# Two-layer hybrid decoder trunk on one core: the low half of the mix reloaded through GpSimd's queue, and the second convolution's taps placed behind the gate's first subtraction

## The chip, the cores and the metric

The kernel runs on one core of a Trainium2 chip. A core has a matrix engine (TensorE, PE in the profile), VectorE (DVE), ScalarE (ACT), GpSimd (POOL) and SyncE (SP); each works through its own list of instructions in order, and the lists are tied together by semaphores. Transfers are started by SP, ACT or POOL and carried out by 16 DMA engines that the core's queues share. The metric is the device time of one execution in microseconds (us), as the median of several runs. A profile is taken of one further execution.

## The reference

Two equal layers on x of 512 tokens by 2048 features. Cut to what matters here:

```python
def _layer(x, norm_g, w_in, conv_w, conv_b, ..., w_out):
    h = _rmsnorm(x, norm_g)
    proj = h @ w_in
    (cv_h, cv_b, cv_c, cv_g, sb_q, sb_k, sb_v, sb_g,
     gl_q, gl_k, gl_v, gl_g, gl_lr) = jnp.split(proj, split_points, axis=-1)
    y_conv = _short_conv(cv_h, cv_b, cv_c, conv_w, conv_b) * silu(cv_g)   # 512 columns
    y_sb = stick-breaking attention of 8 heads * silu(sb_g)               # 1024 columns
    y_gla = rmsnorm(gated linear attention of 4 heads) * silu(gl_g)       # 512 columns
    mix = jnp.concatenate([y_conv, y_sb, y_gla], axis=-1)
    return x + mix @ w_out

def _short_conv(h, b_gate, c_gate, w, bias):
    u = c_gate * h
    y = causal depthwise convolution of u with 3 taps (w)
    return b_gate * (y + bias)
```

All is float32.

## The kernel before, in words

**Products.** A float32 operand is held as a high and a low float16 half, and a product is three float16 products (high by high, high by low, low by high). The halves of the weights are made on the core: a group of 256 weight columns is fetched as float32 (2 MB, tile `st`, two buffers), ScalarE finds its largest square (L383, the "junk" pass, once for each MB), GpSimd takes the maximum over the partitions (L399, tile `wgm`), VectorE makes the scale of it in a few one-column steps (L402 to L417, tiles `wq`, `ws`, `wu`), ScalarE rounds to the high half (`wh`, L454, or L507) and VectorE subtracts for the low half (`wl`, L461, or L508).

**Groups.** A list of weight groups gives the order of the products in each layer: six for the linear attention, four for convolution 0 (h, c, g, b), sixteen for the attention (v, g, q, k of four head pairs), four for convolution 1, and eight output groups of `w_out`. `weights()` takes the next group of the list. At its call the group two further on is fetched by GpSimd's queue (`fetch`, L362), as soon as a `st` buffer is free, that is when the low halves of the group before it are made. With the first and a later matmul of the group it also has the next group's junk pass and its halves placed ("hooks").

**Quick groups.** Some groups are multiplied as 2 by 2 blocks with seven products instead of eight (`project_quick`). It has four partial results in two PSUM banks, `pa` and `pb` in one, `pd` and `pf` in the other (`za`, `zb`, `zd`, `zf` where they are read), which are copied out by ScalarE (L809, L813, L816) and combined by VectorE (L810, L817 to L828), while later products add into the same places. Each product is 24 matmuls of 128 by 256 (L794). The right sides are sums of blocks of the input, tiles `s` (a pair of 2 MB tiles made ahead); the seventh weight part stands in tiles of its own, `w7h` and `w7l`.

**The mix.** The results of the three branches are split in a high and a low half and stored in DRAM (`mixd`), 256 KB for each 128 columns and both halves. The buffers that hold the two halves for the output products are the ones that held the sums `s`, so the reload can begin only when the last quick group of the input, conv g 1, is done with them: the high half (`mix[0]`, an `m` tile) goes over the sums that the fourth of its seven products reads last, the low half (`mix[1]`, the other `m` tile) over those that the product with `wt1` reads. `mixload` issues the reload in three slices of 256, 768 and 512 KB for each half. It is called in `conv_in(1)`, which stands for conv h 1 and conv c 1; `conv_out(1)` then takes conv g 1 (the gate) and conv b 1. After the gate, `weight_ratio` finds one common scale and rescales the halves in place, the high half on ScalarE (L1201), the low half on VectorE (L1202), seven instructions each. Output group 0 (L712, L713, L714) reads them; L714 is the matmul that reads the low half.

**The last attention heads** run in between: their scores are turned by DMA transposes on SP (`th<-za`, L1301), and their products with the values are L1317, 18 matmuls a head. They are called `values(0)` and `values(1)` below. The taps of convolution 1 are two products (L1216), two scalings (L1226) and four shifted multiply-adds (L1228) on VectorE.

**Order.** The program is written in one sequence, and a scheduler that simulates the engines sets the order in each engine's list, with priorities for the weight work. `order(a, b)` only places a behind b.

Of the kernel before, what the change touches and what calls it, by code (L numbers as in the profile page):

```python
# [11 lines left out]
ALU = mybir.AluOpType  # L12
# [31 lines left out]
def hybrid_trunk(ctx, tc, x, norm_g, w_in, conv_w, conv_b, sb_qn_g, sb_kn_g,  # L44
# [132 lines left out]
    def pcol(k, i):  # L177
        return par[:, base[k] + i:base[k] + i + 1]
# [16 lines left out]
    def order(a, b):  # L195
        tc.add_manual_dep(a.ins, b.ins.name, mybir.DependencyInfo(
            mybir.DependencyClass.NoSync, mybir.DependencyReason.DATA), reason="order")
# [248 lines left out]
        else:  # L446
            V.tensor_scalar(wh[:, ks, :GW], staged[0][h][:, ks, :GW], scales[0], None, ALU.mult)

    hooks, lastmm, ksq, added = [], [None], [], [None]

    def whi(i, h):
        wh = wpool.tile([P, HK, GX], F16, tag="wh", name=nm("wh"))
# [83 lines left out]
    def weights():  # L536

        i = cursor[0]
        cursor[0] += 1
        held = names[i][:2] == "v " or names[i] == "conv h 1"  # L540
        if i + 2 < len(specs) and not held:
            with tc.high_priority():
                fetch(i + 2)
        assert not hooks

        def first(mm):
            squares(i + 1, mm)
            if held:
                with tc.high_priority():
                    fetch(i + 2, added[0])  # L550

        if i and i + 1 < len(specs):
            hooks.extend([first, lambda mm: parts_of(i + 1, mm)])
        return loaded.pop(i)
# [130 lines left out]
    for l in range(depth):  # L685
# [89 lines left out]
                parts.extend([a[:, 2 * n], a[:, 2 * n + 1]] for n in range(2))  # L775
            return sums_of((xh, xl), parts, lambda t: [wk([P, HK, P], tag) for tag in ("zw", "zw", "g")])

        def project_quick(src, sums, y, cols, end=None):

            (w11, wT2, w22, wT3, w21, wt1, wT4), u = weights()  # L780
            banks = [bank(psp, "p") for _ in range(3 if end else 2)]
            pa, pb, pd, pf = ([bk[:, n * GW:(n + 1) * GW] for bk in banks for n in range(2)] if not end else
                              [banks[i][:, n * GW:(n + 1) * GW] for i, n in ((0, 0), (0, 1), (1, 0), (2, 0))])
            a11, a12, a22 = ([a[:, 2 * r:2 * r + 2, c::2, :] for a in src] for r, c in ((0, 0), (0, 1), (1, 1)))
            s_, a21_22, a12_s, a11_21 = sums

            def prod(o, w, a, start, stop=False):
                for t in range(1 if cols else 2):
                    for kk in range(HK):
                        for i, (p_, q_) in enumerate(((0, 0), (0, 1), (1, 0))):  # L790
                            st_ = start and t == kk == i == 0
                            en = stop and kk == HK - 1 and i == 2
                            if cols:
                                mm = T.matmul(o, w[q_][:, kk, :], a[p_][:, :, kk, :], start=st_, stop=en,  # L794
                                              skip_group_check=True)
                            else:
                                mm = T.matmul(o[:, t * P:(t + 1) * P], a[p_][:, t, kk, :], w[q_][:, kk, :], start=st_,  # L797
                                              stop=en, skip_group_check=True)
                            if start and t == kk == 0 and i == 2 and o is pa:
                                hook(mm)  # L800
                return mm

            y11, y12, y21, y22 = (
                y[:, c, r * GW:(r + 1) * GW] if cols else y[:, 2 * r:2 * r + 2, c * P:(c + 1) * P]
                for r in range(2) for c in range(2))
            za, zb, zd, zf = (a if cols else a.rearrange("p (t c) -> p t c", c=P) for a in (pa, pb, pd, pf))
            prod(pa, w11, a11, True)
            hook(prod(pb, wT2, s_, False))
            S.activation(y12, za, AF.Copy)  # L809
            V.tensor_tensor(y21, zb, y12, ALU.subtract)  # L810
            prod(pf, w22, a12_s, True)
            prod(pd, wT3, a11_21, end is not None)
            S.activation(y22, zd, AF.Copy)  # L813
            prod(pa, w21, a12, False)
            prod(pb, wt1, a21_22, False, True)
            S.activation(y11, za, AF.Copy)  # L816
            V.tensor_tensor(y12, zb, y12, ALU.subtract)  # L817
            V.tensor_tensor(y22, y12, y22, ALU.subtract)
            if end:
                V.tensor_tensor(y12, zf, y12, ALU.add)  # L820
                end(u, None)
                prod(pd, wT4, a22, False, True)
                end(u, zd)
                return
            lastmm[0] = prod(pd, wT4, a22, False, True)
            V.tensor_tensor(y12, zf, y12, ALU.add)
            yield 0, u
            V.tensor_tensor(y21, zd, y21, ALU.subtract)  # L828
            yield 2, u

        def project(cols, dst):

            if cursor[0] not in quick:
                return project_cols() if cols else project_toks(xh, xl)
            y = dst()
            for _, u in project_quick((xh, xl), insums, y, cols):
                pass
            if cols:
                return [y[:, c, :] for c in range(2)], u
            return [y[:, 2 * b:2 * b + 2, :].rearrange("p a c -> p (a c)") for b in range(2)], u  # L840
# [13 lines left out]
                ps.append(o)  # L854
                yield t, o, u

        def project_gate(mx=None, logistic=False, room=None):

            g = []

            def dst():
                g.append(room or wk([P, 2, seq], "g"))
                return g[0]

            ps, u = project(True, dst)
            quick_ = bool(g)
            g = dst() if not quick_ else g[0]
            top = sm(2, "gtop2") if mx is not None else None
            for c in range(2):
                y = g[:, c, :]  # L870
                if logistic:
                    a = wk([P, seq], "ga") if quick_ else y
                    tables.append(S.activation(a, ps[c], AF.Sigmoid, scale=u))
                    for b in tables[-9:-1]:
                        order(tables[-1], b)
                    if mx is None:
                        V.scalar_tensor_tensor(y, ps[c], u, a, ALU.mult, ALU.mult)
                    else:
                        V.tensor_tensor_reduce(y, ps[c], a, u, 0.28, ALU.mult, ALU.max, top[:, c:c + 1])
                    continue  # L880
                S.activation(y, ps[c], AF.Copy, scale=u)
                a = wk([P, seq], "ga")
                S.activation(a, y, AF.Abs)
                S.activation(a, a, AF.Exp, scale=-1.0)
                S.activation(a, a, AF.Ln, bias=1.0)
                V.scalar_tensor_tensor(a, y, 0.0, a, ALU.min, ALU.subtract)
                tables.append(S.activation(a, a, AF.Exp))
                if mx is None:
                    V.tensor_tensor(y, y, a, ALU.mult)
                else:  # L890
                    V.tensor_tensor_reduce(y, y, a, 1.0, 0.28, ALU.mult, ALU.max, top[:, c:c + 1])
            if mx is not None:
                V.tensor_tensor(mx, top[:, :1], top[:, 1:], ALU.max)
            return g, u
# [29 lines left out]
        def mixload():  # L924

            mix.extend(halves("m", 1 - l))
            for ks in (slice(0, 2), slice(4, 10), slice(12, KT)):
                assert all(k in split for k in range(ks.start, ks.stop))
                for i in range(2):
                    order(nc.sync.dma_start(mix[i][:, :, ks, :], mixd[l][:, i * NT:(i + 1) * NT, ks, :]), lastmm[0])  # L930

# [272 lines left out]
        def conv_in(j, then=lambda: None):  # L1206
# [5 lines left out]
            then()  # L1212
            uc = wk([P, 2, seq], "raw", 1) if j else wk([P, 2, seq], "zw")
            ps, u = project(True, lambda: uc)
            for c in range(2):
                V.scalar_tensor_tensor(uc[:, c, :], ps[c], u, hb[:, c, :], ALU.mult, ALU.mult)  # L1216
            if j:
                mixload()
            y = wk([P, 2, seq], "kT")
            for c in range(2):  # L1220
                ch = 2 * j + c

                def w_(i):
                    return pcol("cw", (l * 3 + i) * 4 + ch)

                V.tensor_scalar(y[:, c, :], uc[:, c, :], w_(2), pcol("cb", l * 4 + ch), ALU.mult, ALU.add)  # L1226
                for d in (1, 2):
                    V.scalar_tensor_tensor(y[:, c, d:], uc[:, c, :seq - d], w_(2 - d), y[:, c, d:], ALU.mult, ALU.add)  # L1228
            then()
            return y, None if j else hb  # L1230

        def conv_out(j, y, room, then=lambda: None):

            g, u = project_gate(logistic=j == 1, room=room)
            V.tensor_tensor(y, y, g, ALU.mult)
            bound = sm(2, "cm")

# [273 lines left out]
```

## Time and profile before

| | |
|---|---|
| median of 3 runs | 1637.63 us (1636.24 to 1638.91) |
| profiled execution, its own time | 1649.88 us |
| span of its profile | 1648.1 us, granted TensorE clock 0.995 |
| busy: PE, DVE, ACT, POOL | 1617.6, 1444.3, 1197.5, 269.8 us |
| DMA traffic | 235.99 MB, 143 GB/s on the mean |

The span runs from the first to the last instruction on the core; the execution's own time has some 2 us around it. A row of the timeline has the start and the duration in us, the engine, the line of the code, the operation, the tile written and the tiles read (out<-in), and in brackets how long the engine had stood idle before it and which tile, made by whom, ended that. Rows of equal instructions are drawn together (x18). SPq is SP's sequencer, which issues transfers. The profiled execution took 12 us longer than the median of the timed runs.

### The profile page before, as it was taken

Reading aid. Unit: us, or ns where it says so; the run is one execution under the profiler, and the core shown is the slowest. Engines: PE = TensorE matmul, PEld = TensorE weight load, DVE = VectorE, ACT = ScalarE, POOL = GpSimd, SP = SyncE. Lnnn points to the kernel's source line nnn. Section 1 sums busy time; section 2 is a strip of 40 time slices with the busy share of each in tenths; the row PEclk is TensorE's granted clock in tenths of the full one; section 3 lists DMA queues with packets and bytes.
Section 4 is the critical chain, followed back from the end, with each engine's and each line's share of the span. In section 5 each row is a group of like instructions: output and inputs, shape, how many; then the busy total and the mean of one; then the engine's idle time right before and its main releaser. Section 6 shows DMA issues by size and latency. Waiting matters only on the chain.

```text
span 1648.1 us, 42250 instructions
## 1 busy us (share of the span) xinstructions
PE 1617.6 (98%) x18202; PEld 1356.3 (82%) x18202; DVE 1444.3 (88%) x2417; ACT 1197.5 (73%) x1771; POOL 269.8 (16%) x300
## 2 busy tenths in 40 slices
PE   7999999999999999999999999999999999989998
PEld 5757768989898967899985768689899998748998
DVE  7989989989898978888698898998989898868896
ACT  8668877968687876666766788787878777755573
POOL 0122021211212121111112112121112112110110
PEclk9999999999999999999999999999999999999999
DMA  7154345476767678445634345456686967693441
GB/s 260 57 125 150 82 124 124 109 158 159 149 158 152 154 159 237 135 156 171 209 99 112 96 116 141 117 135 140 114 199 109 191 121 178 137 232 104 154 155 53
DMA packets 195980, 235.99 MB, mean 143 GB/s; under 512 B 90242, under 2 KB 156108, under 8 KB 195280
## 3 DMA queue, kind: packets, MB, share of 16 engines
q0 software_dynamic: 79072, 178.27, 41.3%
q1 hardware_dynamic: 107712, 45.56, 14.4%
q10 hardware_dynamic: 9008, 9.45, 1.7%
q8 instruction: 142, 2.33, 0.6%
q14 instruction: 46, 0.38, 0.1%
HBM read 179.65 MB, written 14.68 MB: 118 GB/s over the span
## 4 chain that ended last, share of the span: by engine, by line
PE 65%; DVE 21%; ACT 6%; DMA 4%; issue 3%; SPq 1%; POOL 0%; DVEq 0%; ACTq 0%; POOLq 0%
PE psp L797 24%; PE psp L794 14%; PE psp L712 5%; PE psp L713 5%; PE psp L714 5%; DVE wl L508 3%; PE psp L703 3%; PE psp L701 3%; PE psp L702 3%; DVE wl L461 2%; DMA m<-mixd 1%; PE psm L1317 1%; DVE zw L734 1%; PE psz L1277 1%; ACT wh L507 1%
## 5 line engine op out<-in xcount | busy, mean ns | idle before, releaser
L507 ACT ACTIVATE wh<-st,ws 128x1024 f16<-128x1024 f32 x270 | 300.9, 1146 | 176.9 <-DVE st L527 89.9
L508 DVE SCALAR_TENSOR_TENSOR wl<-st,ws,wh 128x1024 f16<-128x1024 f32 x270 | 340.0, 1281 | 28.4 <-ACT wh L507 28.3
L383 ACT ACTIVATE junk<-st 128x2048 uint8<-128x2048 f32 x150 | 285.7, 1905 | 16.6 <-DMA st<-in_w_out_dram 10.0
L794 PE MATMUL psp<-s,wh 128*128 128x256 f16 x1280 | 217.7, 273 | 0.0
L794 PEld LDWEIGHTS <-wh 128*128 128x128 f16 x1920 | 187.4, 98 | 23.3 <-issue 1.4
L714 PE MATMUL psp<-wh,m 128*128 128x256 f16 x640 | 175.9, 275 | 6.9 <-DVE m L1202 6.9
L797 PE MATMUL psp<-wh,s 128*128 128x128 f16 x2048 | 177.2, 219 | 1.6 <-issue 1.5
L712 PE MATMUL psp<-wh,m 128*128 128x256 f16 x640 | 175.8, 275 | 0.6 <-DVE kT L1250 0.6
L713 PE MATMUL psp<-wl,m 128*128 128x256 f16 x640 | 175.8, 275 | 0.0
L794 PE MATMUL psp<-s,wl 128*128 128x256 f16 x640 | 174.3, 273 | 0.9 <-DVE wl L508 0.9
L797 PEld LDWEIGHTS <-s 128*128 128x128 f16 x3072 | 172.9, 98 | 2.0 <-issue 1.7
L797 PE MATMUL psp<-wl,s 128*128 128x128 f16 x1024 | 173.3, 219 | 0.0
L461 DVE SCALAR_TENSOR_TENSOR wl<-st,ws,wh 128x2048 f16<-128x2048 f32 x62 | 144.7, 2347 | 17.4 <-ACT wh L454 17.1
L362 POOL DMA_DIRECT2D st<-in_w_in_dram x114 | 111.1, 1053 | 252.6 <-DVE w7l L508 111.7
L797 PEld LDWEIGHTS <-m 128*128 128x128 f16 x2448 | 139.1, 98 | 2.1 <-issue 1.6
L454 ACT ACTIVATE wh<-st,ws 128x2048 f16<-128x2048 f32 x60 | 118.5, 1997 | 29.9 <-DVE ws L415 20.4
L399 POOL PARTITION_ALL_REDUCE wgm<-wm x75 | 54.4, 725 | 469.7 <-ACT junk L383 454.9
L386 POOL DMA_DIRECT2D st<-st x36 | 57.3, 1591 | 358.3 <-ACT junk L383 339.0
L794 PEld LDWEIGHTS <-wl 128*128 128x128 f16 x960 | 93.9, 98 | 13.2 <-DVE wl L508 1.5
L797 PE MATMUL psp<-wh,m 128*128 128x128 f16 x1088 | 97.2, 219 | 0.4 <-DVE ws L415 0.4
L797 PE MATMUL psp<-wl,m 128*128 128x128 f16 x544 | 93.0, 219 | 0.0
L703 PEld LDWEIGHTS <-wl 128*128 128x128 f16 x384 | 37.6, 98 | 48.0 <-DVE wl L461 3.6
(447 smaller groups left out, 4186.1 us busy)
## 6 DMA issues: line engine op xcount, KB each, us to landing
st<-in_w_in_dram POOLq DMA_DIRECT2D x114, 1024.0 KB, 8.4
st<-in_w_out_dram POOLq DMA_DIRECT2D x32, 1024.0 KB, 9.2
st<-st POOLq DMA_DIRECT2D x36, 512.0 KB, 6.7
st<-in_w_in_dram SPq DMA_DIRECT2D x6, 1024.0 KB, 12.0
mixd<-g POOLq DMA_DIRECT2D x20, 256.0 KB, 7.6
x<-in_x_dram SPq DMA_DIRECT2D x4, 1024.0 KB, 5.0
qT<-in_x_dram ACTq DMA_DIRECT2D x8, 512.0 KB, 6.8
qT<-xs ACTq DMA_DIRECT2D x8, 512.0 KB, 4.2
```

The costliest lines, as they stand in the source:

```text
L362: load = queue.dma_start(s_, src[l, h * HK * P:(h + 1) * HK * P, c0:c0 + GW].rearrange("(k p) n -> p k n", p=P), max_dma_last_dim=1024)
L383: sq = S.activation(junk(HK * GW).rearrange("p (k n) -> p k n", k=part.shape[1]), part, AF.Square, accum_out=peak[i][:, h:h + 1])
L454: hi = S.activation(wh[:, :, :GW], staged[i][h], AF.Copy, scale=scales[i])
L461: V.scalar_tensor_tensor(wl[:, :, :GW], staged[i][h], scales[i], wh[:, :, :GW], ALU.mult, ALU.subtract)
L507: hi = S.activation(h_, b, AF.Copy, scale=sc)
L508: V.scalar_tensor_tensor(l_, b, sc, h_, ALU.mult, ALU.subtract)
L703: mm = T.matmul(o, wl[:, kk, cs], xh[:, :, k, :], start=False, stop=en)
L712: T.matmul(o, ah[:, t, k, :], wh[:, kk, :n], start=st_, stop=False, skip_group_check=True)
L713: T.matmul(o, ah[:, t, k, :], wl[:, kk, :n], start=False, stop=False, skip_group_check=True)
L714: return T.matmul(o, al[:, t, k, :], wh[:, kk, :n], start=False, stop=en, skip_group_check=True)
L794: mm = T.matmul(o, w[q_][:, kk, :], a[p_][:, :, kk, :], start=st_, stop=en, skip_group_check=True)
L797: mm = T.matmul(o[:, t * P:(t + 1) * P], a[p_][:, t, kk, :], w[q_][:, kk, :], start=st_, stop=en, skip_group_check=True)
```

## The change: what it does

1. `mixload` issues the high half on SP's queue as before, and the low half on GpSimd's. The last of the low half's transfers is kept in `reload`, and the fetch of output group 1, which is made at conv b 1, is placed behind it.
2. In conv g 1 alone the fifth and the sixth product change places: `wt1` by `a21_22`, the last reader of the sums under the low half, comes ahead of `w21` by `a12`.
3. The taps of convolution 1 become a closure. It is called inside the gate's `project_quick`, behind the first subtraction on VectorE (L810, `y21 = zb - y12`); its first two instructions are placed behind that subtraction. The values step that stood after the taps in the program now stands ahead of them.

```diff
@@ weights()
-                fetch(i + 2)
+                fetch(i + 2, reload[0] if names[i] == "conv b 1" else None)
@@ project_quick(..., mid=None)
             S.activation(y12, za, AF.Copy)
-            V.tensor_tensor(y21, zb, y12, ALU.subtract)
+            a = V.tensor_tensor(y21, zb, y12, ALU.subtract)
+            if mid is not None:
+                mid(a)
             prod(pf, w22, a12_s, True)
             prod(pd, wT3, a11_21, end is not None)
             S.activation(y22, zd, AF.Copy)
-            prod(pa, w21, a12, False)
-            prod(pb, wt1, a21_22, False, True)
+            if names[cursor[0] - 1] == "conv g 1":
+                prod(pb, wt1, a21_22, False)
+                prod(pa, w21, a12, False, True)
+            else:
+                prod(pa, w21, a12, False)
+                prod(pb, wt1, a21_22, False, True)
@@ mixload()
-                for i in range(2):
-                    order(nc.sync.dma_start(mix[i][:, :, ks, :], mixd[l][:, i * NT:(i + 1) * NT, ks, :]), lastmm[0])
+                for i, q in enumerate((nc.sync, nc.gpsimd)):
+                    a = q.dma_start(mix[i][:, :, ks, :], mixd[l][:, i * NT:(i + 1) * NT, ks, :])
+                    order(a, lastmm[0])
+            reload[0] = a
@@ conv_in(j)
-            for c in range(2):
-                V.scalar_tensor_tensor(uc[:, c, :], ps[c], u, hb[:, c, :], ALU.mult, ALU.mult)
             if j:
                 mixload()
...
+            def taps(behind=None):
+                y = wk([P, 2, seq], "kT")
+                for c in range(2):
+                    a = V.scalar_tensor_tensor(uc[:, c, :], ps[c], u, hb[:, c, :], ALU.mult, ALU.mult)
+                    if behind is not None:
+                        order(a, behind)
...
+            if j:
+                then()
+                return taps, None
+            y = taps()
             then()
-            return y, None if j else hb
+            return y, hb
@@ conv_out(j, taps, room, ...)
+            def mid(behind):
+                made[0] = taps(behind)
+
+            g, u = project_gate(logistic=j == 1, room=room, mid=mid if j else None)
+            y = made[0]
```

The order of GpSimd's list in layer 1, the later kernel against the earlier one, where `st_9488` (`st_9479`) is output group 0, `st_9755` output group 1 and `m_9428` the low half:

```order
 L362 DMA st_9206<-in_w_in_dram 128x8x256 x2
-L399 ISA wgm_9547<-wm_9496 128x2
-L362 DMA st_9488<-in_w_out_dram 128x8x256 x2
+L399 ISA wgm_9538<-wm_9487 128x2
+L362 DMA st_9479<-in_w_out_dram 128x8x256 x2
+L936 DMA m_9428<-mixd_187 128x4x256
+L936 DMA m_9428<-mixd_187 128x4x768
+L936 DMA m_9428<-mixd_187 128x4x512
 L362 DMA st_9755<-in_w_out_dram 128x8x256 x2
```

The three transfers of the low half now stand between the fetches of the two output groups; before, they stood in SP's list behind three transposes.

VectorE's list around conv g 1 of layer 1, before, where `raw_9205` and `kT_9437` are the taps, `wgm_9547` the maximum of conv b 1's weights, and `w7l_9281` the low half of conv g 1's seventh weight part:

```order
992 L1216 SCALAR_TENSOR_TENSOR raw_9205<-raw_9205,wu_9061,qT_9018 128x512 x2
993 L1295 SCALAR_TENSOR_TENSOR zw_9475<-zw_9475,za_9474 128x383
994 L1226 TENSOR_SCALAR kT_9437<-raw_9205,par 128x512
995 L402 TENSOR_TENSOR wq_9546<-wgm_9547 128x1
996 L1226 TENSOR_SCALAR kT_9437<-raw_9205,par 128x512
997 L508 SCALAR_TENSOR_TENSOR w7l_9281<-st_9030,ws_9270,w7h_9280 128x1024
998 L810 TENSOR_TENSOR g_9487<-psp_9491,g_9487 128x256
999 L1228 SCALAR_TENSOR_TENSOR kT_9437<-raw_9205,par,kT_9437 128x511
1000 L411 TENSOR_SCALAR wq_9546<-wq_9546 128x1
```

And now (L1318 to L1346 are the earlier L1293 to L1321; L1229, L1238 and L1240 the earlier L1216, L1226 and L1228):

```order
992 L1320 SCALAR_TENSOR_TENSOR zw_9466<-zw_9466,za_9465 128x383
993 L402 TENSOR_TENSOR wq_9537<-wgm_9538 128x1
994 L411 TENSOR_SCALAR wq_9537<-wq_9537 128x1
995 L415 TENSOR_SCALAR ws_9542<-wq_9537 128x1
996 L417 TENSOR_SCALAR wu_9544<-wq_9537,inoff_156 128x1
997 L508 SCALAR_TENSOR_TENSOR w7l_9281<-st_9030,ws_9270,w7h_9280 128x1024
998 L810 TENSOR_TENSOR g_9478<-psp_9482,g_9478 128x256
999 L1229 SCALAR_TENSOR_TENSOR raw_9205<-raw_9205,wu_9061,qT_9018 128x512 x2
1000 L1324 TENSOR_TENSOR za_9444<-zw_9445,za_9444 128x896
1001 L1324 TENSOR_TENSOR za_9465<-zw_9466,za_9465 128x384
1002 L1238 TENSOR_SCALAR kT_9556<-raw_9205,par 128x512 x2
```

The taps went behind the subtraction L810, and the four scale steps of conv b 1 came ahead of w7l. On ScalarE the two roundings L454 of conv b 1 accordingly moved ahead of the copy L813, behind the second L1298 (a high half of the attention's weights, `za<-zw`).

TensorE's list after `values(0)` of layer 1, before, the seventh product first:

```order
13355 L1317 MATMUL psm_9699<-th_9162,v_7816 128x128
13356 L794 LDWEIGHTS w7h_9280
13357 L794 MATMUL psp_9492<-x_185,w7h_9280 128x256
13358 L794 LDWEIGHTS w7l_9281
13359 L794 MATMUL psp_9492<-x_185,w7l_9281 128x256
```

And now, the product with `wt1` first, into the bank that L810 reads:

```order
13355 L1342 MATMUL psm_9699<-th_9162,v_7816 128x128
13356 L794 LDWEIGHTS wh_9278
13357 L794 MATMUL psp_9482<-s_1133,wh_9278 128x256
13358 L794 LDWEIGHTS wl_9279
13359 L794 MATMUL psp_9482<-s_1133,wl_9279 128x256
```

Before, ten of the seventh product's 24 matmuls, the product with `w21`, that with `wt1` and the rest of the seventh followed each other. Now they run whole, `wt1`, `w21`, then the seventh. The 18 matmuls of `values(1)`, of which one stood early in conv b 1 and 17 at its end, all stand at its end. Layer 2 has the same moves in all these places.

More of the change, by code (lines that the diff above doesn't have):

```diff
@@ L447, in whi0 @@
             V.tensor_scalar(wh[:, ks, :GW], staged[0][h][:, ks, :GW], scales[0], None, ALU.mult)
-    hooks, lastmm, ksq, added = [], [None], [], [None]
+    hooks, lastmm, ksq, added, reload = [], [None], [], [None], [None]
     def whi(i, h):
@@ L776, in xsums, with project_quick @@
             return sums_of((xh, xl), parts, lambda t: [wk([P, HK, P], tag) for tag in ("zw", "zw", "g")])
-        def project_quick(src, sums, y, cols, end=None):
+        def project_quick(src, sums, y, cols, end=None, mid=None):
             (w11, wT2, w22, wT3, w21, wt1, wT4), u = weights()
@@ L829, in project_quick, with project @@
             yield 2, u
-        def project(cols, dst):
+        def project(cols, dst, mid=None):
             if cursor[0] not in quick:
@@ L835, in project @@
             y = dst()
-            for _, u in project_quick((xh, xl), insums, y, cols):
+            for _, u in project_quick((xh, xl), insums, y, cols, mid=mid):
                 pass
@@ L855, in project_by_token, with project_gate @@
                 yield t, o, u
-        def project_gate(mx=None, logistic=False, room=None):
+        def project_gate(mx=None, logistic=False, room=None, mid=None):
             g = []
@@ L863, in dst @@
                 return g[0]
-            ps, u = project(True, dst)
+            ps, u = project(True, dst, mid)
             quick_ = bool(g)
@@ L1214, in conv_in, with w_, conv_out @@
             ps, u = project(True, lambda: uc)
-            for c in range(2):
-                V.scalar_tensor_tensor(uc[:, c, :], ps[c], u, hb[:, c, :], ALU.mult, ALU.mult)
             if j:
                 mixload()
[L1219 to L1228, printed above, removed]
-            then()
-            return y, None if j else hb
-        def conv_out(j, y, room, then=lambda: None):
-            g, u = project_gate(logistic=j == 1, room=room)
+            def taps(behind=None):
[4 more added lines that the diff above has]
+                        order(a, behind)
+                for c in range(2):
+                    ch = 2 * j + c
+                    def w_(i):
+                        return pcol("cw", (l * 3 + i) * 4 + ch)
+                    V.tensor_scalar(y[:, c, :], uc[:, c, :], w_(2), pcol("cb", l * 4 + ch), ALU.mult, ALU.add)
+                    for d in (1, 2):
+                        V.scalar_tensor_tensor(y[:, c, d:], uc[:, c, :seq - d], w_(2 - d), y[:, c, d:], ALU.mult,
+                                               ALU.add)
+                return y
+            if j:
+                then()
+                return taps, None
+            y = taps()
+            then()
+            return y, hb
+        def conv_out(j, taps, room, then=lambda: None):
+            made = [None if j else taps]
+            def mid(behind):
+                made[0] = taps(behind)
+            g, u = project_gate(logistic=j == 1, room=room, mid=mid if j else None)
+            y = made[0]
             V.tensor_tensor(y, y, g, ALU.mult)
```

## The prediction

> **What bounds the kernel now.** I read the page first, then the waits of TensorE, then the rows around conv gate 1 (the group where the change sits) in both layers, then the queues beside them.
>
> ```profile
> span 1648.1 us, 42250 instructions
> PE 1617.6 (98%) x18202; PEld 1356.3 (82%) x18202; DVE 1444.3 (88%) x2417; ACT 1197.5 (73%) x1771; POOL 269.8 (16%) x300
> ```
>
> TensorE is busy 98% of the span, so only its 30.5 idle us, or work taken from it, can be won; the change takes no matmul away. Next, what ended its idle times (total, times, longest):
>
> ```profile
> PE psp L714 <- DVE m L1202: 6.9, 2, 4.1
> ...
> PE psp L794 <- DVE w7l L508: 1.9, 2, 1.1
> ...
> PE psm L1317 <- DMA th<-za: 0.9, 1, 0.9
> ```
>
> The w7l wait stands once in each layer, the other two once in the program. TensorE in layer 1 and then layer 2 (start, duration, in brackets the idle time before the row):
>
> ```profile
> 636.12 1.81 PE L1317 MATMUL psm<-th,v 128*128 128x256 f16 x18
> 638.07 0.27 PE L794 MATMUL psp<-x,w7h 128*128 128x256 f16 x1
> 639.21 0.28 PE L794 MATMUL psp<-x,w7l 128*128 128x256 f16 x1 [0.87 <-DVE w7l L508]
> ...
> 646.97 0.38 PE L701 MATMUL psp<-x,wh 128*128 128x512 f16 x1
> ```
> ```profile
> 1441.61 1.81 PE L1317 MATMUL psm<-th,v 128*128 128x256 f16 x18
> 1443.30 0.27 PE L794 MATMUL psp<-m,w7h 128*128 128x256 f16 x1
> 1444.65 0.28 PE L794 MATMUL psp<-m,w7l 128*128 128x256 f16 x1 [1.08 <-DVE w7l L508]
> ...
> 1452.41 0.38 PE L701 MATMUL psp<-m,wh 128*128 128x512 f16 x1
> ```
>
> After the values step the seventh product starts, finds its low weights missing, and stops. Three products of 24 matmuls stand between the values and the next group: from the second matmul (639.21) to conv b 1's first (646.97) are 71 steps in 7.76 us, 0.109 us each, so 72 without a stall take 7.87 us. Conv b 1 could start at 645.94 and 1451.17: the stall costs 646.97 - 645.94 = 1.03 us in layer 1 and 1.24 us in layer 2.
>
> The largest wait is at output group 0 of layer 2, on VectorE's rescaling of the low half of the mix (TensorE, then VectorE and its twin of layer 1, then both layers' group 0 by windows):
>
> ```profile
> 1480.34 0.40 PE L714 MATMUL psp<-wh,m 128*128 128x256 f16 x1 [4.09 <-DVE m L1202]
> 1480.52 0.42 PE L712 MATMUL psp<-wh,m 128*128 128x256 f16 x1
> ...
> 1488.90 0.42 PE L713 MATMUL psp<-wl,m 128*128 128x256 f16 x1
> ```
> ```profile
> 666.20 3.33 DVE L1202 TENSOR_SCALAR m<-m,ratio 128x1024 f16<-128x1024 f16 x7
> ...
> 1489.12 0.88 DVE L1202 TENSOR_SCALAR m<-m,ratio 128x1024 f16<-128x1024 f16 x2 [3.47 <-DMA m<-mixd]
> ```
> ```profile
> 669.30:690.60 21.30, 21.30 (x199) 19.11 (x198) 17.23 (x22) 14.92 (x16) 0.40 (x1) 1.00 0.28 98
> 1475.80:1507.50 31.70, 24.18 (x194) 19.84 (x192) 19.08 (x27) 17.22 (x19) 2.17 (x3) 0.84 0.35 118
> ```
>
> The same group takes 21.3 us in layer 1, without a wait and at clock 1.00, and 31.7 in layer 2, at clock 0.84 (last columns: clock, DMA share, GB/s). With the 0.89 us ahead of it the episode costs 31.7 - 21.3 + 0.9 = 11.3 us. Its source is a stretch in which the transfers crawl: at 1459 the DMA engines were busier than in layer 1 and moved a fifth of the bytes:
>
> ```profile
> 1459.00:1469.00 10.00, 10.00 (x48) 4.53 (x47) 4.10 (x8) 8.34 (x8) 0.40 (x1) 1.00 1.50 64
> 652.00:662.00 10.00, 10.00 (x48) 4.51 (x46) 6.37 (x9) 8.41 (x7) 0.40 (x1) 1.00 1.02 310
> ```
>
> **Against which time.** The profiled execution took 1649.88 us, the timed median is 1637.63 (1636.24 to 1638.91). 1649.88 - 11.3 = 1638.6, inside the timed range. I read this so: the crawl is in the profiled execution and not, or hardly, in the timed ones. So the 11.3 us, most of what the profile offers this change, is not in the time I must forecast.
>
> **The change part by part.**
>
> Swap of the last two products on conv gate 1, and the taps behind the gate's first subtraction. VectorE before the seventh product, layer 1:
>
> ```profile
> 635.11 1.39 DVE L1216 SCALAR_TENSOR_TENSOR raw<-raw,wu,qT 128x512 f32<-128x512 f32 x2
> ...
> 636.88 0.54 DVE L1226 TENSOR_SCALAR kT<-raw,par 128x512 f32<-128x512 f32 x1
> 637.34 0.15 DVE L402 TENSOR_TENSOR wq<-wgm 128x1 f32<-128x1 f32 x1
> ...
> 637.87 1.28 DVE L508 SCALAR_TENSOR_TENSOR w7l<-st,ws,w7h 128x1024 f16<-128x1024 f32 x1
> 639.06 0.42 DVE L810 TENSOR_TENSOR g<-psp,g 128x256 f32<-128x256 f32 x1
> ...
> 640.12 1.09 DVE L1299 TENSOR_TENSOR za<-zw,za 128x896 f16<-128x896 f32 x1
> ...
> 641.78 0.56 DVE L1299 TENSOR_TENSOR za<-zw,za 128x384 f16<-128x384 f32 x1
> ```
>
> Before, the first product of the taps and two scalings (L1226, the second like the first) stood ahead of w7l, 1.39 + 2 x 0.54 = 2.47 us; now they come after L810, and the four scale steps of conv b 1 (L402 to L417, 0.15 us each, which I put at 0.1 apart) stand there, the first bound by the maximum that GpSimd finishes at 635.36 + 0.74 = 636.10 (GpSimd, layer 1, and its last row layer 2):
>
> ```profile
> 635.36 0.74 POOL L399 PARTITION_ALL_REDUCE wgm<-wm  x1 [16.59 <-ACT junk L383]
> 639.45 1.79 POOL L362 DMA_DIRECT2D st<-in_w_out_dram  x2 [3.35 <-DVE w7l L508]
> 650.17 1.76 POOL L362 DMA_DIRECT2D st<-in_w_out_dram  x2 [8.93 <-DVE wl L461]
> ...
> 1440.23 0.61 POOL L399 PARTITION_ALL_REDUCE wgm<-wm  x1 [15.97 <-ACT junk L383]
> ```
>
> So w7l starts at about 636.5 and L810 at 637.7, done at 638.1. The seventh product now comes 48 matmuls (5.2 us) after the values, at 643.3: w7l's cover is over 5 us. But the product that now follows the values adds into the PSUM bank that L810 reads, so TensorE waits for L810 instead: until 638.17 against 638.07, 0.1 us in layer 1. In layer 2 the maximum is there at 1440.84, so L810 is done 2.0 us later, at 1442.9, 0.4 us ahead of the product at 1443.30: nothing. Gain 1.03 - 0.10 + 1.24 = 2.17, rounded 2.2 us.
>
> What else stands in the way of those 72 matmuls: the seventh product's bank is copied out first by ScalarE (L813), which now stands behind two weight roundings L454. Those waited for the scale until 643.10:
>
> ```profile
> 637.17 0.57 ACT L1298 ACTIVATE za<-zw 128x384 f16<-128x384 f32 x1
> ...
> 643.10 3.90 ACT L454 ACTIVATE wh<-st,ws 128x2048 f16<-128x2048 f32 x2 [5.08 <-DVE ws L415]
> ...
> 652.98 1.91 ACT L383 ACTIVATE junk<-st 128x2048 uint8<-128x2048 f32 x1 [2.19 <-DMA st<-in_w_out_dram]
> ```
>
> With the scale at 636.5 they run from 637.7, after the L1298 that they now follow, to 641.6, and L813, a copy as small as L810, to about 642.0: 1.3 us ahead of 643.3. Conv b 1's low weights take
>
> ```profile
> L461 DVE SCALAR_TENSOR_TENSOR wl<-st,ws,wh 128x2048 f16<-128x2048 f32 x62 | 144.7, 2347 | 17.4 <-ACT wh L454 17.1
> ```
>
> 2.35 us, and on VectorE now follow L810, the taps' 2.47 us and the two L1299: 638.1 + 2.5 + 1.65 + 2.35 = 644.6, ahead of TensorE's need at 646. Both are covered; uncovered, each us late is one lost.
>
> The taps themselves (these four instructions and four shifted ones) move towards the stretch where VectorE has room, 3.6 of 10 us from 652 (its 6.37 busy in the window above), and are needed only when the gate is done: nothing. The values step of the second block leaves conv b 1's start as well; the same 18 matmuls run before or after: nothing, and their transposes get later deadlines.
>
> The low half's three transfers leave SP for GpSimd. SP's issues, layer 1 and then layer 2:
>
> ```profile
> 640.53 9.75 SPq L1301 DMA_TRANSPOSE th<-za x3
> 650.37 3.12 SPq L930 DMA_DIRECT2D m<-mixd x3
> ...
> 1460.75 7.54 SPq L930 DMA_DIRECT2D m<-mixd x3
> ```
>
> Before, they stood behind three transposes until 650.4 and 1460.8. Now they wait on GpSimd for the low-half product, which ends two products sooner in the order (638.17 + 24 x 0.109 = 640.8). Three issues by the pair's 1.79 / 2 = 0.9 us each end near 643.5; behind them GpSimd has only the fetch of output group 1, which waits for conv b 1's L461 anyway (650.17 before). Hidden in layer 1, whose low half was never waited for; in layer 2 the same, without the crawl. Bounds of this part in the timed runs: 0 (they had no such wait) and -11.3 (they had all of it). I take 0, being nearest to the layer 1 rows.
>
> By the Trainium skill (DMA: Bandwidth & Descriptors, "Issuing engines are not separate DMA queues") a transfer runs on the same 16 engines whoever starts it, and another issuer saves only issue time; by it the queue change is worth nothing here, as in my sum, and it would not cure a crawl. The same page ("Queues, rings and completion order") has each engine take a queue's descriptors in ring order; the low half then runs after group 0's weights and ahead of group 1's instead of beside them. No row here shows a mix transfer in that queue.
>
> Fetch of group 1 behind the low half: costs at most the 3.1 us that group 1's landing is late, and its weights are due 21 us later. At output group 0 VectorE now takes group 1's scale ahead of the sums for the later groups (they start later by about one junk pass, 1.91 us). Those sums feed products of group 1, after TensorE's 21.3 us on group 0, of which VectorE is busy 17.23: room for 4 us. I take 0, with 1.9 us a layer as the upper end.
>
> Sum: 1637.63 - 2.2 = 1635.4. Against the profiled execution: 1649.88 - 2.2 = 1647.7 with the crawl's stall, 1636.4 without.
>
> **Rivals.**
>
> A: the timed runs carry part of the layer 2 episode, and it goes. For: the transfers' delay is real, and the three runs spread over 2.7 us. Against: 1638.6 above. Time: 1635.4 less 1 to 11, half of it 1630. It is also the case in which the profile after gains more than 10 us.
>
> B, on the other side: the low half delays group 0's weights. ScalarE already waits 2.19 us for their second part (652.98), and the maximum found there opens the chain to the scales, the ratio and TensorE's group 0, with about 2 us to spare. If the low half's 1.5 MB shares the engines with those 2 MB instead of following them, at 310 GB/s the weights land 1.5 MB / 310 = 4.8 us later, less 1.4 for their earlier issue: TensorE loses 3.4 - 2 = 1.4 us a layer, 2.8 in all, 1638.2; if the spare time is gone as well, 6.8: 1642.2. It decides when they land over 3.4 us late. The wait of 4.09 us halved the clock here (28 matmuls of 0.42 us, 0.213 apart instead of 0.109: 2.9 us more); the one of 1.08 left them 0.109 apart. By the Trainium skill (TensorE: Matmul & The Clock Gate, "What's actually happening") an idle window of about 3.4 us is what halves it; by that rule B's waits would cost only themselves.
>
> C: the swap does not pay: TensorE meets L810, or L813 behind the roundings, as late as it met w7l. Then the 2.2 us stay: 1637.6. Against: the spare times above.
>
> **How the numbers follow.** A difference under 0.2% (3.3 us) can't be told from none here. My forecast (gain 1 to 3 us) has 0.58, A 0.20, B 0.13, C 0.09. Time 1635.4. The low end is A at more than half, 1629.0; the high end is halfway through B, 1640.0: beyond them lie a quarter of A and a third of B and some scatter, under 2 in 10. Faster by over 0.2% needs 1634.35 or less: most of A and the upper edge of my case, 0.32. Slower needs 1640.9: half of B, 0.07. Same 0.61.
>
> **What would show it.** Right: no wait on w7l in either layer; conv b 1's first matmul 9.5 to 10.0 us after the start of the values step (before 10.85 and 10.80); the low half's transfers on GpSimd, issued 5 us after the values step and landed by about 657 in layer 1; group 0 without a wait on L1202. Wrong: a wait of TensorE on L810 of over 0.5 us, or on L813; the junk pass of group 0's second part later than 653; a new wait at group 0. A time under 1632 would say that the timed runs did carry the layer 2 stall.

## The result, and the profile after

The changed kernel takes 1635.42 us, the median of 21 runs (1634.85 to 1638.14). Before, run beside it 21 times, takes 1639.26 us (1636.24 to 1650.32). The ratio is 0.997, with a 95% interval from 0.9955 to 0.9984: 0.3% faster. The time is the one forecast, 1635.4; what moved is before. Of its 21 runs 3 take 1647 to 1651 us, and the other 18 have a median of 1638.64, 1.0 us above the three runs shown with the profile before (median 1637.63). With the runs of before taken beside the experiments, 28 of 108 take over 1642 us; of 33 runs of the change none reaches 1639.

The page after, span and engines, and the first waits of TensorE (this execution took 1638.14 us, the longest of the 21):

```profile
span 1636.3 us, 42257 instructions
PE 1615.8 (99%) x18202; PEld 1356.5 (83%) x18202; DVE 1445.4 (88%) x2417; ACT 1197.3 (73%) x1771; POOL 274.1 (17%) x306
```
```profile
PE psz L244 <- ACT qp L234: 3.1, 1, 3.1
PE psp L703 <- DVE wl L461: 2.1, 2, 1.3
```

The three waits that the prediction rested on (L714 on the low half, w7l, the last `th`) are gone; those that are left stand elsewhere, and the two shown were there before (3.0 and 2.2 us). TensorE around conv gate 1, layer 1 and layer 2 (L1342 is the earlier L1317):

```profile
637.92 1.81 PE L1342 MATMUL psm<-th,v 128*128 128x256 f16 x18
639.77 0.27 PE L794 MATMUL psp<-s,wh 128*128 128x256 f16 x1
...
647.63 0.38 PE L701 MATMUL psp<-x,wh 128*128 128x512 f16 x1
```
```profile
1442.53 1.81 PE L1342 MATMUL psm<-th,v 128*128 128x256 f16 x18
1444.37 0.27 PE L794 MATMUL psp<-s,wh 128*128 128x256 f16 x1
...
1452.23 0.38 PE L701 MATMUL psp<-m,wh 128*128 128x512 f16 x1
```

From the values step to conv b 1 it is 647.63 - 637.92 = 9.71 us and 1452.23 - 1442.53 = 9.70 us, against 10.85 and 10.80 before: 1.14 and 1.10 us, 2.24 us together. VectorE, GpSimd and SP beside it in layer 1:

```profile
638.11 1.27 DVE L508 SCALAR_TENSOR_TENSOR w7l<-st,ws,w7h 128x1024 f16<-128x1024 f32 x1
639.31 0.42 DVE L810 TENSOR_TENSOR g<-psp,g 128x256 f32<-128x256 f32 x1
```
```profile
639.68 1.78 POOL L362 DMA_DIRECT2D st<-in_w_out_dram  x2 [2.46 <-DVE w7l L508]
642.85 2.36 POOL L936 DMA_DIRECT2D m<-mixd  x3 [1.39 <-PE psp L794]
649.74 1.76 POOL L362 DMA_DIRECT2D st<-in_w_out_dram  x2 [4.53 <-DVE wl L461]
```
```profile
640.14 1.67 SPq L936 DMA_DIRECT2D m<-mixd  x3
642.07 22.37 SPq L1326 DMA_TRANSPOSE th<-za  x3
```

L810 ends at 639.73, 0.04 us ahead of the product that reads its bank at 639.77. The low half is issued at 642.85, behind group 0's weights. SP spends 22 us on three transposes, more than before (9.75), and nobody waits: the values of the second block now stand at the end of conv b 1, at 668.35. It is close: in the trace the packets of these transposes stand behind the high half and pass from 664.1 to 667.6. The crawl of layer 2 is gone (64 GB/s before in this window), and output group 0 takes the same in both layers (before 21.30 and 31.70):

```profile
1459.00:1469.00 10.00, 10.00 (x48) 4.53 (x47) 8.42 (x20) 6.15 (x7) 0.77 (x2) 1.00 1.07 311
```
```profile
669.90:691.10 21.20, 21.20 (x198) 19.01 (x197) 15.86 (x18) 12.83 (x14) 0.40 (x1) 1.00 0.20 67
1474.40:1495.60 21.20, 21.20 (x198) 19.02 (x197) 16.62 (x20) 14.23 (x15) 0.40 (x1) 1.00 0.24 83
```

### The profile page after: what moved, and what is told of

It is laid out like the page before. It is cut to its first block, busy times and chain, and to the rows that moved or that the text cites. A ratio compares the mean times of both kernels' runs of the same rounds, so it can differ in the third digit from the quotient of the medians.

```text
span 1636.3 us, 42257 instructions
## 1 busy us (share of the span) xinstructions
PE 1615.8 (99%) x18202; PEld 1356.5 (83%) x18202; DVE 1445.4 (88%) x2417; ACT 1197.3 (73%) x1771; POOL 274.1 (17%) x306
## 4 chain that ended last, share of the span: by engine, by line
PE 69%; DVE 17%; ACT 7%; DMA 4%; issue 3%; POOL 0%; SPq 0%; DVEq 0%; ACTq 0%; POOLq 0%
PE psp L797 23%; PE psp L794 17%; PE psp L712 4%; PE psp L713 4%; PE psp L714 4%; PE psp L703 3%; PE psp L702 3%; PE psp L701 3%; DVE wl L508 3%; PE psp L856 2%; DMA st<-in_w_in_dram 2%; DVE wl L461 2%; PE psm L1342 2%; PE psz L1302 1%; DVE zw L734 1%
## 5 line engine op out<-in xcount | busy, mean ns | idle before, releaser
L714 PE MATMUL psp<-wh,m 128*128 128x256 f16 x640 | 174.5, 273 | 0.0
L461 DVE SCALAR_TENSOR_TENSOR wl<-st,ws,wh 128x2048 f16<-128x2048 f32 x62 | 145.0, 2349 | 16.1 <-ACT wh L454 15.4
L454 ACT ACTIVATE wh<-st,ws 128x2048 f16<-128x2048 f32 x60 | 118.6, 1999 | 20.9 <-DVE ws L415 11.8
```

Of the source, the lines that this page charges most:

```text
L454: hi = S.activation(wh[:, :, :GW], staged[i][h], AF.Copy, scale=scales[i])
L461: V.scalar_tensor_tensor(wl[:, :, :GW], staged[i][h], scales[i], wh[:, :, :GW], ALU.mult, ALU.subtract)
L714: return T.matmul(o, al[:, t, k, :], wh[:, kk, :n], start=False, stop=en, skip_group_check=True)
```

## The experiments

The edits are against before unless said, and cut to the lines that matter. Theory 1 at the start: the w7l stall is worth 2.2 us in every run, and the reload takes away only what single runs wait for. Its rivals gave the whole gain to one part. "Before" is always the kernel before on the same chip and in the same hours.

### The reload's part alone (twice)

```diff
-                fetch(i + 2)
+                fetch(i + 2, reload[0] if names[i] == "conv b 1" else None)
...
-                for i in range(2):
-                    order(nc.sync.dma_start(mix[i][:, :, ks, :], mixd[l][:, i * NT:(i + 1) * NT, ks, :]), lastmm[0])
+                for i, q in enumerate((nc.sync, nc.gpsimd)):
+                    a = q.dma_start(mix[i][:, :, ks, :], mixd[l][:, i * NT:(i + 1) * NT, ks, :])
+                    order(a, lastmm[0])
+            reload[0] = a
```

> Only the reload's part: the low half on GpSimd's queue and the fetch of output group 1 behind it; products and taps as before. My theory (the w7l stall is worth 2.2 us in every run, the reload only takes away what is waited for in some runs): TensorE keeps the waits on w7l, about 1.9 us in all, and conv b 1 starts 10.8 us after the start of the values step in both layers; no wait on the rescaled low half; best runs as those of before (1636 to 1637), median 1637 to 1638, no run over 1642. Rival (the whole gain comes from the reload): the time of the change, 1635.4.

> Only the reload's part again, beside the change on one chip. Theory 1 (the w7l stall is worth 2.2 us in every run, and the rest of the change's gain is the reload's): median 1.8 to 2.6 us over the change's, and 1 to 2 us under that of before, with no run over 1642. Rival (the reload's part has the whole gain): the same median as the change within 0.5 us.

> The change itself, on the same chip as the next kernel: 1635 to 1636, none over 1639.

First 1638.37 us (1636.56 to 1641.44) against 1641.31 of before, ratio 0.9969 (0.9945 to 0.9992); again 1637.71 (1636.31 to 1639.9) against 1640.5, ratio 0.9978 (0.9957 to 0.9999). The change beside the second took 1635.77 (1634.7 to 1636.81), ratio 0.996 (0.9937 to 0.9984). TensorE's waits with the reload's part alone (first run) keep the stall:

```profile
PE psp L794 <- DVE w7l L508: 2.1, 2, 1.1
```

So the change is made of two parts: 1637.71 - 1635.77 = 1.94 us (95% interval 1.1 to 2.9, resampled from 12 runs each) for taps and swap, as forecast, and 2.8 us at the median for the reload, with no run of the 24 over 1642. The second is known less well: the ratio's interval (0.9957 to 0.9999) leaves 0.2 to 7 us. Most of it is the slow runs of before: without those over 1642 (9 of 23 and 10 of 29) its medians are 1638.57 and 1638.33, only 0.2 and 0.6 us above the reload's part alone. Theory 1 had the first part right and the second too small.

### The swap alone

```diff
-            prod(pa, w21, a12, False)
-            prod(pb, wt1, a21_22, False, True)
+            if names[cursor[0] - 1] == "conv g 1":
+                prod(pb, wt1, a21_22, False)
+                prod(pa, w21, a12, False, True)
+            else:
+                prod(pa, w21, a12, False)
+                prod(pb, wt1, a21_22, False, True)
```

> Only the two products of conv g 1 change places; the lists of all engines but TensorE stay word for word. My theory: the low weights of the seventh part get 5 us of cover, but the product that now comes first needs VectorE's subtraction L810, which still stands behind the taps and ends at 639.48 against 638.07: the wait of 1.0 to 1.1 us on w7l turns into one of about 1.4 us on L810 in each layer; conv b 1 starts 11.0 to 11.2 us after the start of the values step; the time is that of before or 0.5 us more. Rival (the swap alone hides w7l): 9.7 us, and 2.2 us less time than before.

1640.27 us (1635.75 to 1653.51), ratio 0.9996 (0.9968 to 1.0025): nothing, as expected, but by another way. TensorE:

```profile
637.89 0.27 PE L794 MATMUL psp<-x,w7h 128*128 128x256 f16 x1
639.07 0.28 PE L794 MATMUL psp<-x,w7l 128*128 128x256 f16 x1 [0.91 <-DVE w7l L508]
```

The scheduler leaves the seventh product first after the values, presumably because L810 is late in its simulation as well; the swapped pair only follows. The wait on w7l stays, and the one on L810 that I expected doesn't come.

### The taps alone, and taps with swap, the low half left on SP

```diff
 the change without its edits of mixload and weights(); the first also without the swap
```

> Only the taps behind the gate's subtraction; reload on SP and products as before. My theory: this part alone removes the w7l wait, since w7l is made 1.2 us or more earlier; conv b 1 starts 9.7 us after the start of the values step; 2.2 us less than before in the best runs (1634.0 to 1635); runs with a late low half, some of 1645 and more, remain possible. Rival (the taps help only together with the swap): conv b 1 keeps 0.5 us or more of a wait.

> Taps and swap, the reload of the low half left on SP. My theory: 9.7 us from the values step to conv b 1, best runs as those of the change (1634.9), but the low half still stands behind transposes on SP, so the spread of before (up to 1640 and single runs of 1648 to 1650) stays. Rival (the spread comes from elsewhere, or goes with the compute part): runs as narrow as those of the change, 1634.9 to 1638.

1661.4 us (1656.72 to 1669.79), ratio 1.0109 (1.007 to 1.0148), and 1667.6 us (1665.28 to 1673.82), ratio 1.0151 (1.0114 to 1.0188). Both sides' expectations fell: the part that I had worth -2.2 us costs 20 to 26 when it comes without the other. With the taps alone the w7l stall is gone, and in its place (waits of TensorE; L1204 and L1336 are the earlier L1202 and L1317):

```profile
PE psp L714 <- DVE m L1204: 9.4, 4, 5.2
PE psm L1336 <- DMA th<-za: 7.8, 4, 3.3
```

With taps and swap it is `th` alone. In layer 1 the last transpose stands behind the low half on SP there (issued at 664.86), and TensorE waits 10.90 us for it:

```profile
PE psm L1340 <- DMA th<-za: 23.6, 3, 12.4
```

SP, GpSimd and the windows of the run with the taps alone, layer 1:

```profile
641.51 15.98 SPq L1320 DMA_TRANSPOSE th<-za  x3
657.59 15.14 SPq L932 DMA_DIRECT2D m<-mixd  x3
```
```profile
649.13 1.75 POOL L362 DMA_DIRECT2D st<-in_w_out_dram  x2 [8.22 <-DVE wl L461]
```
```profile
654.00:660.00 6.00, 6.00 (x29) 2.73 (x28) 5.87 (x8) 5.22 (x5) 0.00 (x0) 1.00 1.03 58
```

The crawl of the profile before (DMA engines full, 58 GB/s) is now in layer 1 too. One thing stands out: group 1's fetch at 649.13 starts 12.1 us after the values step (637.00) instead of 14.05, because L461 that frees its buffer comes sooner, and it starts while the transposes are still on SP. Before, layer 1 had the transposes through SP at 640.53 + 9.75 = 650.28 and the fetch at 650.17, next to no overlap; layer 2 had 1445.63 + 15.02 = 1460.65 and the fetch at 1455.62, 5 us of overlap, and crawled:

```profile
1445.63 15.02 SPq L1301 DMA_TRANSPOSE th<-za  x3
```
```profile
1455.62 1.76 POOL L362 DMA_DIRECT2D st<-in_w_out_dram  x2 [8.94 <-DVE wl L461]
```

### The taps alone, with group 1's fetch held until the transposes have landed

```diff
 against the taps alone
-                fetch(i + 2)
+                fetch(i + 2, turned[0] if names[i] == "conv b 1" else None, True)
```

`turned` is the last transpose; with the last argument `fetch` makes its transfers wait for it.

> The kernel with only the taps moved (reload of both halves on SP, products as before), and the fetch of output group 1 held until the last transpose of the second block has landed. Theory 1 (the transposes crawl and the low half is late because group 1's weights, fetched 1.9 us sooner after the values step, now run beside the transposes): transposes through SP by 12 us after the values step, under 2 us of slow packets, no wait on the low half, 1635 to 1638. Theory 2 (the crawl comes from the order on SP's queue alone: high half, transposes, low half): slow packets and waits as with the taps alone, 1652 or more.

1635.44 us (1633.7 to 1637.4), ratio 0.9949 (0.9924 to 0.9973). One wait on one fetch takes away 26 us (before stood at 1641.31 beside the one and 1640.5 beside the other), with both halves of the mix on SP in the old order; GpSimd's maximum for group 0 goes ahead of the held fetch with it. It is level with the change beside it (1635.77), so nothing here beats the change clearly. SP is through its transposes 16.5 us after the values step, not 12 as I expected. SP, GpSimd and the windows:

```profile
641.55 11.93 SPq L1323 DMA_TRANSPOSE th<-za  x3
653.57 1.63 SPq L935 DMA_DIRECT2D m<-mixd  x3
```
```profile
658.24 1.78 POOL L362 DMA_DIRECT2D st<-in_w_out_dram  x2 [4.12 <-DMA th<-za]
```
```profile
654.00:660.00 6.00, 6.00 (x29) 2.74 (x28) 5.75 (x8) 5.31 (x5) 1.88 (x3) 1.00 1.10 236
```

So in the kernel with the taps alone it is group 1's weights beside the transposes that cost the 26 us: take the overlap away, and they go. Group 1's weights, 9 us later, are still in time. The overlap alone isn't enough: with the reload's part alone (first run) the transposes' packets pass from 653.4 to 667.3, beside the low half and group 1's weights on GpSimd's queue; the engines move 308 GB/s from 652 to 666, and nobody waits.

### The change without the swap

> The change without its swap of two products: taps behind the subtraction, low half on GpSimd's queue, fetch behind it. The low half's last reader is then the second product after the values step, not the first, so its transfers start 24 x 0.109 = 2.6 us later. Theory 1 (the swap only moves the low half 2.6 us, and that half had 10 us to spare): no wait on w7l, none on the rescaled low half, the time of the change, 1635 to 1636.5, 2 to 4 us below before. Rival (the earlier start is what keeps the low half out of trouble): a wait of TensorE on the rescaled low half again, 1640 or more.

1635.71 us (1634.68 to 1637.71), ratio 0.9973 (0.9956 to 0.999): the swap is worth nothing that can be measured, alone or here. This kernel is also the one with the taps alone plus the reload's part: to take the low half off SP, with group 1's fetch behind it, cures the 26 us just as the held fetch does.

### The change with other queues

```diff
 against the change, and the last against before
-                for i, q in enumerate((nc.sync, nc.gpsimd)):
+                (nc.gpsimd, nc.gpsimd)   both halves on GpSimd
+                (nc.sync, nc.scalar)     low half on ScalarE
+                (nc.gpsimd, nc.sync)     high half on GpSimd, low half on SP
+                (nc.gpsimd, nc.sync)     the same in before, products and taps as there
```

> The change, with the high half's transfers on GpSimd's queue too, so that SP carries nothing but the transposes there. Theory 1 (the transfers crawl where copies of the mix stand behind transposes on SP's queue): no crawl, values for the second block landed early, the time of the change or up to 1 us less (1634.5 to 1636.5). Theory 2 (transposes crawl wherever they run beside 4 KB loads, and on SP they were only held back behind the high half): the transposes now run beside the weights from the start, the crawl moves to about 4 us after the values step, the weights of group 0 land late, 1645 or more.

> The change, with the low half's transfers issued by ScalarE instead of GpSimd. Theory 1 (it matters only that the low half doesn't stand behind the transposes on SP's queue): no wait on the rescaled low half; time of the change plus at most 1 us for what ScalarE waits: 1635 to 1637. Rival (it has to be GpSimd's queue, where it runs in turn between the two groups' weights): the low half or the weights land late and 1640 or more.

> The change with the two halves' queues exchanged: the high half on GpSimd's queue, the low half on SP behind all transposes of the second block. Theory 1 (copies of the mix behind transposes on SP are what crawls and is waited for): as the runs that left the low half on SP, 1655 or more, TensorE waiting for the low half's rescaling in both layers. Rival (what hurts is the compute part's order together with both halves on one queue): with the halves on two queues the time stays below 1640.

> Before, with the high half's transfers on GpSimd's queue and the low half left on SP behind the transposes; products and taps as before. Theory 1 (either half off SP is enough, since then no transpose stands behind a copy of the mix, or no copy behind a late transpose): as with only the reload's part, 1636 to 1639 and no run over 1642, hardly any slow packet of the transposes. Rival (it is the low half that has to leave SP): the tail of before stays, single runs of 1645 to 1650.

Both on GpSimd: 1635.36 us (1634.09 to 1639.3), ratio 0.9973 (0.9957 to 0.9988). The transposes do run beside the weights from the start, and they are slow: their packets pass until 667.0, 1.2 us ahead of the values step that needs them (668.24). But the weights aren't slowed with them (306 GB/s from 643 to 667), so the late weights and the 1645 us of theory 2 don't come.

Exchanged, within the change: 1636.07 us (1634.15 to 1638.78), ratio 0.9984 (0.9969 to 0.9998). Theory 1 had 1655 or more and fell: in this kernel the low half may stand behind all transposes on SP, with the high half not ahead of them. SP in layer 1:

```profile
637.92 10.32 SPq L1326 DMA_TRANSPOSE th<-za  x4
648.34 12.36 SPq L936 DMA_DIRECT2D m<-mixd  x3
```

The four transposes are issued by 648.24, ahead of group 1's fetch, but that is SP's part only: in the trace their packets pass until 664.0, beside the high half and both groups' weights, and nobody waits (298 GB/s from 642 to 664). So the costly case of this order of the work had three things together: the high half ahead of the transposes on SP, group 1's weights beside them, the low half behind them. Each was taken away in one run (here, the held fetch, the change without the swap), and each time the kernel took 1635.4 to 1636.1 us.

Exchanged, within before: 1682.01 us (1670.91 to 1688.42), ratio 1.0234 (1.019 to 1.0278), where I expected 1636 to 1639 and the rival the tail of before. TensorE and SP, layer 1:

```profile
652.23 0.28 PE L1317 MATMUL psm<-th,v 128*128 128x256 f16 x1 [4.29 <-DMA th<-za]
672.70 2.40 PE L1317 MATMUL psm<-th,v 128*128 128x256 f16 x12 [20.18 <-DMA th<-za]
```
```profile
637.38 19.05 SPq L1301 DMA_TRANSPOSE th<-za  x4
```

GpSimd now issues the high half ahead of group 0's weights (at 636.56), and the transposes crawl beside them (146 GB/s from 641 to 647). The lists moved too: of the 18 matmuls of the second values step 13 now stand behind the second matmul of conv b 1 (one in before, none in the change), where they need `th` some 20 us sooner. How much of the 42 us is these early matmuls, and how much the later transposes, no run separates. So this run doesn't say whether the high half may leave SP in place of the low half.

Low half on ScalarE: 1642.08 us (1639.47 to 1645.59), ratio 1.0007 (0.9989 to 1.0026). Its first waits, and ScalarE and VectorE in layer 1:

```profile
PE psp L701 <- DVE g L823: 4.8, 2, 2.9
```
```profile
648.99 4.42 ACTq L936 DMA_DIRECT2D m<-mixd  x2
653.46 0.72 ACT L925 ACTIVATE m<-e,bsmix 128x512 f16<-128x512 f32 x1 [11.83 <-DMA m<-mixd]
654.09 0.36 ACT L822 ACTIVATE g<-psp 128x256 f32<-128x256 f32 x1
```

Not the low half is late but ScalarE: the first of its three issues starts at 640.74, the last ends at 653.41, and they hold the copy L822 (before L816), VectorE's L823 and the bank that conv b 1's products need. I had put that at 1 us or less; against the change without the swap it is 6.4. So the time is the rival's (1640 or more), for another reason than the rival gave. On GpSimd the same issue took 2.36 us, and nothing that was due soon stood behind it.

## Why the prediction was right or wrong

- **w7l and the taps: right, with one term too small.** Forecast 1.03 - 0.10 and 1.24, measured in the profile 1.14 and 1.10, in the runs 1.94. From the maximum to L810's end I had 2.0 us; in layer 1 of the profile it was 2.51 (637.22 to 639.73), and it was covered only because the maximum came 0.70 us ahead of the values step instead of 0.02. In the second profile of the change it came 0.11 behind, and TensorE waits for L810 (row below), just over the 0.5 us that I had named as a sign of being wrong; conv b 1 starts 10.24 us after the values step there, a gain of 0.61 in place of 1.14, and layer 2 keeps its 9.71. ScalarE's L813 and conv b 1's low weights were covered: no wait on either. That it was the taps and not the swap, I hadn't separated: the swap is worth nothing.

```profile
639.37 0.27 PE L794 MATMUL psp<-s,wh 128*128 128x256 f16 x1 [0.57 <-DVE g L810]
```

- **The cover of that part: missed.** I took taps and swap as worth 2.2 us by themselves, and costed group 1's fetch only as one that lands later, behind the low half (3.1 us at most); I did not ask what an earlier one collides with. In layer 1 before, that fetch started when the transposes had just gone; 1.9 us sooner, with the taps alone, it makes them crawl, and the kernel takes 20 us more. In the change the two hardly meet, which I had not worked out: the high half shares the engines with the low half and group 1's weights, the transposes behind it on SP pass from 664.1 on, and group 1 has landed by 666.9.
- **The reload's part: mis-sized.** I took 0, from 1638.6 lying within the timed range. It is 2.8 us at the median beside the second run of the reload's part. None of the three runs shown lies over 1642, but 28 of 108 do, and no run of the reload's part (24) or of the change (33). That was the premise of rival A, which I gave 0.20; its time, 1630, didn't come, because the three runs that it started from had nothing to lose. The bound -11.3 that I kept fits the tail (1650.32 - 1638.6). (The wait on L714 stands twice in layer 2, 4.09 and 2.86 us, not once; the 11.3 counts both.)
- **The time to the tenth: luck in part.** With 28 in 108 over 1642, three runs without one come about four times in ten. The 1637.63 happened to be about what the kernel takes with the reload's part alone (1637.71 and 1638.37), so 2.2 less was the time of the change; the gain over before was 3.84, not 2.2.
- **Rival B: not so.** Group 0's second part was ready for its junk pass 13.0 us after the values step began (row below), before 16.9; queue order held: in the trace the weights of group 0 land by 650.9, the low half by 652.3, 656.1 and 658.9 (I had about 657), group 1 by 662.7 and 666.9. The Trainium skill's ring order (DMA: Bandwidth & Descriptors, "Queues, rings and completion order") agrees. Its rule that another issuer saves only issue time ("Issuing engines are not separate DMA queues") is right in its words and misled me in its size: the same page calls that time small, and here SP stood 16 us on three transposes. The low half moved to GpSimd, with group 1's fetch behind it, made 1635.7 of 1661.4 us; how much of that is issue time and how much the new order of the transfers, no run separates.

```profile
650.95 1.91 ACT L383 ACTIVATE junk<-st 128x2048 uint8<-128x2048 f32 x1 [1.69 <-DMA st<-in_w_out_dram]
```

- **The chances.** 0.61 on no difference was too much: the ratio lies beyond 0.2% (its interval reaches to 0.16%), because the change was measured against a before that is 1.6 us slower than the three runs.

## What to carry to other kernels

A profiled execution that is slower than the timed median by the size of one stall may show a stall that a quarter of the runs have; ask for more runs before it is set to zero. When an edit makes an engine finish sooner, look up which buffer that frees and which transfer then starts, and what that transfer runs beside. A transfer that others queue behind is best kept short or alone on its queue, and its consumer placed late in the list.

## What the runs showed of the hardware

Three transposes of the attention's weights hold SP for 9.75 us in one kernel (before, layer 1) and for 22.37 us in another (the change), and what SP has to issue behind them starts that much later. A row of SP ends with the issue; the packets can come long after (exchanged queues: issued by 648.24, last packet at 664.0).

Where the transposes' packets of 256 bytes are alone, 580 of them pass in a us (fetch held, 654 to 656). Beside GpSimd's queue, with packets of 3 to 4.6 KB, 64 pass for 56 of the others (both halves on GpSimd, 654 to 660). In the crawl it is 36 for 11.5 (taps alone, 654 to 660): both queues are slowed.

In the crawl a packet of 256 bytes takes 195 to 380 ns (medians over 2 us), against 18 ns at the median of both layers' stretches. Over these stretches 688 of them took over 100 ns in the profile before, 637 with the taps alone, 99 with the reload's part alone, 73 with the change, 42 with the fetch held, and 8 and 9 in the two changed kernels where no copy of the mix stood ahead of them on SP. What slows a single packet isn't settled. Weights run beside the transposes in every crawl, but also without one (the reload's part alone, the exchanged queues in the change). A copy ahead of them in SP's queue is there in every crawl but that of the exchanged queues in before, where only the weights and the high half on another queue were.
